# One core, a two-layer decoder step: the order of TensorE's instructions in the mixing stage

## The chip, the core and the metric

One core of a Trainium2 chip runs the whole program. The metric is the device time of one execution in microseconds (us). TensorE multiplies (its weight loads are listed apart, as PEld), VectorE (DVE), ScalarE (ACT) and GpSimd (POOL) do the elementwise work, and SyncE's queue (SP) issues nearly all DMAs. The kernel is written in a framework that takes the text of the program and then orders the instructions of each engine itself: it plays the program through with an own timing model and gives a free engine the earliest instruction of the text that is ready in that model. The order so made is fixed before the program runs; on the chip each engine works through its list.

## What is computed

Two layers, each with a SwiGLU block, a token mixing block and a second SwiGLU block, all with RMS norms. Tokens are 512 of a prompt and 8 x 8 of samples that continue a cache of 2048. The mixing block, cut to what matters:

```python
z = hn @ w_in_l                                   # 1024 -> 3584 = 28 items of 128 columns
aq, ak, av, bq, bf, bi, bg = split(z)             # attention q k v, then HGRN2 q f i g
outs = [dilated_window(aq, ak, av, w, d) for (w, d) in ((128, 1), (512, 4), (2048, 16))]
o_a = rmsnorm(dilated_mixture(outs), attn_g)      # softmax weights over three patterns
f = lb + (1 - lb) * sigmoid(bf);  qh = silu(bq)   # HGRN2, per head:
S_t = diag(f_t) S_{t-1} + (1 - f_t) outer i_t;  o_t = S_t^T qh_t
o_b = rmsnorm(o_t, hgrn_g) * silu(bg)
out = concat(o_a, o_b) @ w_out_l
```

The prompt starts its HGRN2 state at zero, the samples from a stored state; new keys, values and states are outputs too.

## The kernel before

Tokens lie in two halves of 288 columns (256 of the prompt, 32 of samples), `hf` 0 and 1. Every weight product is one **item** of 128 output columns; for each half it is 24 matmuls of 128 x 288 (8 tiles of the contraction, three products each, since weights and operands are split into a high and a low part; lines 353 to 355 in `product`). `run_phase` issues the items of a phase in order, both halves of an item one after the other in the mixing stage. `w_split` (lines 114 and 116) prepares weights ahead, `w_dma` (line 95) loads them.

The **mixing stage** (`mixing`) has 28 items of the input projection: 0 to 7 queries and keys, 8 to 11 values, 12 to 23 for HGRN2 head 0 to 3 in threes (forget gate, query, input), 24 to 27 the output gates. After each item and half, `evac` reads the product from PSUM and then `side` takes steps of the other work, all written as Python generators:

- `sample` (4 steps each time): attention of the samples, four pairs of sequences. Of each pair ten steps of scores (`sc`, line 849; each step reads two `kv` tiles of 256 KB that `kv_load`, lines 815 and 818, fetches into a ring of KVB = 5), one step with the new keys (`scn`) and the exponential (line 875), three of transposes (`ptps`, line 884), and for each sequence eleven products with the values (`pov`, line 904), a copy (line 910) and a transpose back (`otr`, line 913).
- `hgrn` (2 steps of each of up to two heads): eight steps of small products (`lev`, lines 590 to 631), after each of which DVE and POOL rescale `zq` and `zk` (lines 601, 639 to 661), which the next step reads; then `ktp`, `kv`, `pos`, `po`, `snew`, and the norm (`stat`, `bc`).
- `prompt` (2 steps): 16 units, each with four steps: scores (`psc`, line 765) and softmax, scaling, transposes (`ptp`, line 780, copied by ACT at line 784 and by DVE at line 782), product with the values (`ppv`, line 789).

PSUM has two buffers each for weight products (`ps_mm`), HGRN2 (`ps_hg`), samples (`ps_sa`) and prompt (`ps_pr`). Tiles of the pool `tmp` have six buffers; an output gate (items 24 to 27) holds one in the list `gates` until its head is done and `gate_outputs` uses it. Once the last item is there, `rest` goes round the generators until nothing is left, and `w_out` follows with eight items from another pool of PSUM. `rest` is also called from the middle of item 27's second half, by `hook` and `o_chain`.

The text thus says: 24 matmuls, then up to some ten small steps, then 24 matmuls, and so on. In which order TensorE takes them is the framework's choice: it may take a matmul of the next item while a step of a head waits for DVE.

Of the kernel before, what the change touches and what calls it, by code (L numbers as in the profile page):

```python
# [9 lines left out]

F32 = mybir.dt.float32
F32R = mybir.dt.float32r
U8 = mybir.dt.uint8
AF = mybir.ActivationFunctionType
ALU = mybir.AluOpType
# [32 lines left out]
def trunk_step(ctx: ExitStack, tc: tile.TileContext, a, L):  # L48
# [13 lines left out]
    ps_mm = ctx.enter_context(tc.tile_pool(name="ps_mm", bufs=2, space=PSUM))  # L62
    ps_hg = ctx.enter_context(tc.tile_pool(name="ps_hg", bufs=2, space=PSUM))

# [1 line left out]
    items = []  # L66
    for l in range(L):
        ff = {}
# [56 lines left out]
        while st["dma"] < min(st["split"] + 2, len(items)):  # L125
            w_dma()

# [1 line left out]
    def const(name, shape):  # L129
        return cp.tile(shape, F32, name=name)  # L130

# [34 lines left out]
    def late_consts():  # L166
        lstage = tmp("lstage")[:, :NLM * 32].rearrange("p (a b) -> p a b", b=32)
        for n, t in (("logits", logit), ("lmask", lstage), ("pbias", pbias), ("sb_str", sb_str), ("sb_rec", sb_rec),
                     ("sb_new", sb_new), ("bmask", bmask), ("eye32", eye32)):
            sp.dma_start(t if n == "lmask" else t[:], a[n])  # L170
        dve.tensor_copy(lmask[:], lstage)
        # lower bounds of the forget gates
        dve.tensor_copy(lbm[:], logit[:, 0, :])
        for l in range(1, L):
            dve.tensor_tensor(lbm[:], lbm[:], logit[:, l, :], op=ALU.max)
        for l in range(L):
            dve.tensor_tensor(lbe[:, l, :], logit[:, l, :], lbm[:], op=ALU.subtract)
        act.activation(lbe[:], lbe[:], AF.Exp)
        dve.tensor_copy(lbs[:], lbe[:, 0, :])
        for l in range(1, L):  # L180
            dve.tensor_tensor(lbs[:], lbs[:], lbe[:, l, :], op=ALU.add)
        dve.reciprocal(lbs[:], lbs[:])
        for l in range(L):
            dve.tensor_tensor(lbe[:, l, :], lbe[:, l, :], lbs[:], op=ALU.mult)
        dve.tensor_copy(lbm[:], lbe[:, 0, :])
        for l in range(L):
            if l:
                dve.tensor_tensor(lbm[:], lbm[:], lbe[:, l, :], op=ALU.add)
            dve.tensor_tensor(fof[:, l, :], lbm[:], lbe[:, 0, :], op=ALU.subtract)
            dve.tensor_scalar(fsc[:, l, :], fof[:, l, :], -0.5, 0.5, op0=ALU.mult, op1=ALU.add)  # L190
            dve.tensor_scalar(nfs[:, l, :], fsc[:, l, :], -1.0, None, op0=ALU.mult)
            dve.tensor_tensor(fof[:, l, :], fof[:, l, :], fsc[:, l, :], op=ALU.add)
# [2 lines left out]
    def tmp(name="tmp"):  # L195
        return tp.tile([P, H], F32, name=name, tag="tmp", bufs=6)

# [1 line left out]
    def stats(acc, inv, out_psum=False, tag="rb"):  # L199
        """rsqrt of the mean square of every token, on all partitions: [128, 288]"""  # L200
        s = ps_hg.tile([P, 512], F32, name="stat", tag="hg")
        for c in range(3):
            pe.matmul(s[:96, c:c + 1], acc[:, 96 * c:96 * c + 96], ones[:, 0:1], start=True, stop=True)
        sm = tp.tile([96, 4], F32, name="sm", tag="sm", bufs=2)
        dve.tensor_scalar(sm[:, :3], s[:96, :3], inv, EPS, op0=ALU.mult, op1=ALU.add)
        pool.tensor_tensor(sm[:, :3], sm[:, :3], nhalf[:96, :3], op=ALU.pow)  # L206
        yield
        b = ps_hg.tile([P, 512], F32, name="bc", tag="hg")
        for c in range(3):
            pe.transpose(b[:, 96 * c:96 * c + 96], sm[:, c:c + 1].to_broadcast([96, P]), ident[:96, :96])  # L210
        if out_psum:
            return b[:, :H]
        rb = tp.tile([P, H], F32, name="rb", tag=tag, bufs=1)
        act.activation(rb[:], b[:, :H], AF.Copy)
        return rb[:]

    class Chain:
        """what one half of the tokens goes through between two phases, issued in steps: jn tiles of the
        next operand are there, then its scale r"""

        def __init__(self, hf, gen):
            self.hf, self.jn, self.r, self.done = hf, 0, None, False
# [116 lines left out]
            c()  # L339

    def product(group, order=None, chain=None):
        """group: (psum, item, high, low); one tile of the contraction after the other, for all of them"""
        for _, i, _, _ in group:
            w_get(i)
        k = items[group[0][1]][1]
        order = order or range(k)
        for n, j in enumerate(order):
            s = slice(j * P, (j + 1) * P)
            if chain is not None:
                chain.until(n + 1)  # L350
            for ps, i, xhi, xlo in group:
                wh, wl = whi[i], wlo[i]
                pe.matmul(ps, wh[:, s], xhi[:, j, :], start=(n == 0), stop=False)  # L353
                pe.matmul(ps, wh[:, s], xlo[:, j, :], start=False, stop=False)  # L354
                pe.matmul(ps, wl[:, s], xhi[:, j, :], start=False, stop=(n == k - 1))  # L355
            if len(group) > 1 or n == k // 2 - 1:
                hook()

    def run_phase(n, operand, evac, chains, order=None, lag=LAG, side=None, on_done=None):
        """n items from items[st.next]; operand(i, hf) gives (psum, high, low), evac(i, hf, psum) takes the product"""  # L360
        i0 = st["next"]
        st["next"] += n

        def issue(idx, hf):
            group, tiles = [], []
            if idx[0] == 0:
                chains[hf].until(1)
            for i in idx:
                pst, xhi, xlo = operand(i, hf)
                group.append((pst[:, :H], i0 + i, xhi, xlo))  # L370
                tiles.append(pst)
            first = idx[0] == 0
            product(group, order if first else None, chains[hf] if first else None)
            flush_late()
            if hf == 0:
                w_ahead(i0 + idx[-1])
            else:
                w_ahead(i0 + idx[0])
            hook()
            if first:  # L380
                chains[hf].until_r()
            for i, pst in zip(idx, tiles):
                evac(i, hf, pst)
                if i == n - 1 and on_done is not None:
                    active.append(on_done(hf))
                if side is not None:
                    side(i, hf)

        g = list(range(GRP))
        issue(g, 0)  # L390
        issue(g, 1)
        for i in range(GRP, n):
            issue([i], 0)
            if i - lag >= GRP:
                issue([i - lag], 1)
        for i in range(max(GRP, n - lag), n):
            issue([i], 1)
        flush_late()

# [1 line left out]
    def swiglu(l, w, chains, gp, mk_chain, side=None):  # L401
        with ExitStack() as es:
            hpool = es.enter_context(tc.tile_pool(name="hid", bufs=1))
# [60 lines left out]
            run_phase(n, operand, evac, chains, side=side, on_done=on_done)  # L464
        return nxt

# [1 line left out]
    def mixing(l, chains, xpool_close, x_spill):  # L468
        o = [None, None]
        with ExitStack() as es:  # L470
# [39 lines left out]
            def evac(i, hf, pst):  # L510
                ps = pst[:, :H]
                r = rn[hf]
                if i < 8:
                    dst = (aq if i < 4 else ak)[:, i % 4, hf, :]
                    dve.tensor_tensor(dst, ps, r, op=ALU.mult)
                    if i == 7 and hf == 1:
                        late.append(lambda: sp.dma_start(a["o_k"][l], ak[:]))
                    return
                t = tmp("z")
                if i < 12 or (i < 24 and i % 3 == 2):  # L520
                    dve.tensor_tensor(t[:], ps, r, op=ALU.mult)
# [27 lines left out]
                    gates.append((h, hf, t))  # L549

            gates = []
            left = [12, 12]
            gated = [0, 0]
            normed = [False, False]
# [9 lines left out]
            hg_done = set()  # L564
            stage = [0] * 4

# [1 line left out]
            def pcol(t, c):  # L568
                return t[:, c // 2, (c % 2) * P:(c % 2) * P + P]

# [163 lines left out]
                hg_done.add(h)  # L734
                stage[h] = 4

# [1 line left out]
            def prompt_unit(p, i, alt):  # L738
                n = (i + 1) * P
                if alt == 1:  # L740
# [58 lines left out]
                    yield from prompt_unit(p, i, alt)  # L799
                    left[i // 2] -= 1  # L800

# [1 line left out]
            kvq = []  # L803
            kvs = {"n": 0}

# [132 lines left out]
            def side(i, hf):  # L938
# [10 lines left out]
                if i < 8:  # L949
                    return  # L950
                if i == 11 and hf == 1:
                    flush_late()
                    flags["av"] = True
                    prm.append(prompt(0))
# [17 lines left out]
                        if not pull(g):  # L972
                            hg.remove(g)

# [1 line left out]
            oa_g = g_of(l, "attn_norm_g")  # L976

            def anorm(hf):
# [43 lines left out]
            oc = [o_chain(0), o_chain(1)]  # L1022
            run_phase(28, operand, evac, chains, lag=0, side=side, on_done=lambda hf: oc[hf])
            tail["on"] = True
            while hg or prm or smp or alt or alt2 or an or gates:
                rest()
        return oc

    def w_out(l, chains, gp, mk_chain):
# [24 lines left out]
            run_phase(NJ, operand, evac, chains, on_done=on_done)  # L1054
        return nxt

# [1 line left out]
    xs = ExitStack()  # L1058

    def x_tiles():  # L1060
# [44 lines left out]
    xs.close()  # L1105


# [1 line left out]
def _tiles(w):  # L1109
    """(..., K, M) -> (..., M/128, 128, K): one contiguous [128, K/128 * 128] block for every 128 columns"""  # L1110
    *b, K, M = w.shape
    n = len(b)
    t = w.reshape(*b, K // P, P, M // P, P)
# [2 lines left out]


def _cols(v):
    """(L, n*128) -> (128, L, n)"""
    L = v.shape[0]  # L1120
    return np.transpose(v.reshape(L, -1, P), (2, 0, 1))

# [93 lines left out]
```

## Time and profile before

| | us |
|---|---|
| runs | 2618.42, 2623.82, 2625.37 (median 2623.82) |
| profiled execution, first to last instruction | 2620.2 |
| layer 0, item 12's first matmul to `w_out`'s first | 539.8 to 823.5 |
| layer 1, the same | 1837.5 to 2124.0 |

Busy times of TensorE add up the modelled lengths of overlapping matmuls (0.29 us each, one every 0.13 us), so a piece of work on it is best taken from start to start in the timeline. "idle before" in a row is time in which the engine had nothing to do, with the instruction that ended it. A weight matmul is 128 x 288; a name such as `sc<-kv,qbd` gives the tile written and those read, "x4" counts instructions merged into the row.

### The profile page before, as it was taken

How to read it: one execution, taken by the hardware profiler on the slowest of the kernel's cores; microseconds unless marked ns; L12 is line 12 of the kernel's file. 1: busy time of each engine (PE TensorE's matmuls, PEld its weight loads, DVE VectorE, ACT ScalarE, POOL GpSimd, SP SyncE). 2: the span in 40 equal slices, each digit the busy share in tenths (PEclk: the TensorE clock that was granted, in tenths of full speed). 3: DMA queues.
4: the chain of work that ended last, by engine and by line, in shares of the span. 5: the costliest groups of instructions: out<-in, count | busy, mean ns of one | idle time of the engine just before them, and what ended most of it. 6: DMA issues, size and time to landing. Idle time of an engine off the chain costs nothing.

```text
span 2620.2 us, 52041 instructions
## 1 busy us (share of the span) xinstructions
PE 2570.6 (98%) x21844; PEld 2401.9 (92%) x21844; DVE 1186.3 (45%) x2648; ACT 900.4 (34%) x2023; POOL 384.0 (15%) x450
## 2 busy tenths in 40 slices
PE   8999999999999999999999999999999999999997
PEld 8999999867878999999999999997677799999997
DVE  6333346235555642434563334362456556324333
ACT  5232235133335532223532322342333254323232
POOL 1101012002212210101210010110022122101012
PEclk9999999999999999999999999999999899999998
DMA  5222223475543222222222222236754442222221
GB/s 177 81 81 81 89 74 109 159 240 172 167 155 130 82 89 81 83 87 76 78 89 81 81 81 89 74 108 190 223 186 156 131 145 73 87 83 74 89 81 44
DMA packets 108604, 292.03 MB, mean 111 GB/s; under 512 B 12753, under 2 KB 16081, under 8 KB 107601
## 3 DMA queue, kind: packets, MB, share of 16 engines
q1 hardware_dynamic: 107936, 288.28, 34.0%
q8 instruction: 172, 2.82, 0.4%
q14 instruction: 64, 0.52, 0.1%
q10 hardware_dynamic: 432, 0.41, 0.1%
HBM read 272.13 MB, written 16.52 MB: 110 GB/s over the span
## 4 chain that ended last, share of the span: by engine, by line
PE 90%; DVE 4%; issue 3%; DMA 1%; POOL 1%; ACT 1%; SPq 0%; POOLq 0%; ACTq 0%; DVEq 0%
PE gu L353 13%; PE gu L354 13%; PE gu L355 13%; PE mm L353 12%; PE mm L355 12%; PE mm L354 12%; PE sc L849 2%; PE pov L904 1%; PE psc L765 1%; PE ppv L789 1%; DMA kv<-in_kc 1%; DVE y L313 1%; POOL sm L206 1%; PE ptp L780 1%; DVE x L316 1%
## 5 line engine op out<-in xcount | busy, mean ns | idle before, releaser
L353 PE MATMUL gu<-xh,whi 128*128 128x288 f32 x2752 | 813.3, 296 | 7.1 <-ACT xh L269 6.3
L354 PE MATMUL gu<-xl,whi 128*128 128x288 f32 x2752 | 813.1, 295 | 0.0
L355 PE MATMUL gu<-xh,wlo 128*128 128x288 f32 x2752 | 811.2, 295 | 0.0
L114 ACT ACTIVATE whi<-wraw 128x512 fp32r<-128x512 f32 (+1 forms) x688 | 394.9, 614 | 758.3 <-PE gu L354 360.6
L116 DVE TENSOR_TENSOR wlo<-wraw,whi 128x512 fp32r<-128x512 f32 (+1 forms) x688 | 445.3, 680 | 194.7 <-ACT whi L114 176.9
L353 PEld LDWEIGHTS gu<-xh,whi 128*128 128x128 f32 x2752 | 517.9, 188 | 8.3 <-ACT xh L269 6.7
L355 PEld LDWEIGHTS gu<-xh,wlo 128*128 128x128 f32 x2752 | 518.9, 189 | 0.0
L354 PEld LDWEIGHTS gu<-xl,whi 128*128 128x128 f32 x2752 | 517.7, 188 | 0.5 <-DVE xl L270 0.5
L353 PE MATMUL mm<-hh,whi 128*128 128x288 f32 x1408 | 415.7, 295 | 0.0
L355 PE MATMUL mm<-hh,wlo 128*128 128x288 f32 x1408 | 414.7, 295 | 0.0
L354 PE MATMUL mm<-hl,whi 128*128 128x288 f32 x1408 | 414.7, 295 | 0.0
L434 POOL TENSOR_TENSOR gate<-gate,rb 128x288 f32<-128x288 f32 x176 | 163.8, 931 | 1287.8 <-ACT gate L433 1287.8
L353 PE MATMUL mm<-xh,whi 128*128 128x288 f32 x1088 | 334.9, 308 | 1.5 <-DVE y L449 1.5
L354 PE MATMUL mm<-xl,whi 128*128 128x288 f32 x1088 | 327.3, 301 | 0.0
L355 PE MATMUL mm<-xh,wlo 128*128 128x288 f32 x1088 | 327.3, 301 | 0.0
L355 PEld LDWEIGHTS mm<-hh,wlo 128*128 128x128 f32 x1408 | 264.7, 188 | 0.0
L354 PEld LDWEIGHTS mm<-hl,whi 128*128 128x128 f32 x1408 | 264.4, 188 | 0.0
L353 PEld LDWEIGHTS mm<-hh,whi 128*128 128x128 f32 x1408 | 264.2, 188 | 0.0
L438 DVE TENSOR_TENSOR hid<-gu,gate 128x288 f32<-128x288 f32 x172 | 78.7, 457 | 332.2 <-PE gu L355 323.6
L353 PEld LDWEIGHTS mm<-xh,whi 128*128 128x128 f32 x1088 | 205.3, 189 | 25.1 <-issue 21.4
L354 PEld LDWEIGHTS mm<-xl,whi 128*128 128x128 f32 x1088 | 205.4, 189 | 12.9 <-issue 12.4
L355 PEld LDWEIGHTS mm<-xh,wlo 128*128 128x128 f32 x1088 | 205.6, 189 | 12.6 <-issue 12.1
(193 smaller groups left out, 2430.0 us busy)
## 6 DMA issues: line engine op xcount, KB each, us to landing
wraw<-in_wgu SPq DMA_DIRECT2D x175, 512.0 KB, 3.4
kv<-in_kc SPq DMA_DIRECT2D x160, 256.0 KB, 3.4
kv<-in_vc SPq DMA_DIRECT2D x160, 256.0 KB, 3.3
wraw<-in_wd SPq DMA_DIRECT2D x64, 448.0 KB, 3.3
wraw<-in_w_in SPq DMA_DIRECT2D x56, 512.0 KB, 4.2
wraw<-in_wd SPq DMA_DIRECT2D x32, 512.0 KB, 3.5
wraw<-in_w_out SPq DMA_DIRECT2D x16, 512.0 KB, 4.4
xs<-x SPq DMA_DIRECT2D x4, 1152.0 KB, 4.2
```

Of the source, the lines that this page charges most:

```text
L114: act.activation(whi[i][:, c], r[:, c], AF.Copy)
L116: dve.tensor_tensor(wlo[i][:, c], r[:, c], f(whi[i][:, c]), op=ALU.subtract)
L206: pool.tensor_tensor(sm[:, :3], sm[:, :3], nhalf[:96, :3], op=ALU.pow)
L313: ins = dve.tensor_tensor(y[:, js, :], y[:, js, :], rb[:, None, :].to_broadcast([P, 2, H]), op=ALU.mult)
L316: dve.tensor_tensor(x[:, js, :], x[:, js, :], y[:, js, :], op=ALU.add)
L353: pe.matmul(ps, wh[:, s], xhi[:, j, :], start=(n == 0), stop=False)
L354: pe.matmul(ps, wh[:, s], xlo[:, j, :], start=False, stop=False)
L355: pe.matmul(ps, wl[:, s], xhi[:, j, :], start=False, stop=(n == k - 1))
L434: pool.tensor_tensor(g[:], g[:], rn[hf], op=ALU.mult)
L438: dve.tensor_tensor(h[:], ps, gate[hf][:], op=ALU.mult)
L765: pe.matmul(dst, q, kk, start=True, stop=True, tile_position=(64 * s, 0))
L849: pe.matmul(ps[32 * p:32 * p + 32, c], qbd[:, 2 * bp + bb, p, :], rhs(p), start=(bb == 0), stop=(bb == 1), tile_position=(0, 32 * p))
```

## The change

A guard for the order by hand opens in `side` after item 11's second half and covers TensorE alone; it closes when the stage is done. What lies in it goes to TensorE's list in the order of the text. The other engines' lists, and TensorE's outside of it, are ordered as before. In `evac` an item from 24 on first runs `rest` while three or more gates wait in `gates`. Comments and docstrings are blanked. The core:

```diff
+END = 1
...
                 return
+                while i >= 24 and len(gates) >= 3:
+                    rest()
                 t = tmp("z")
...
             gates = []
+            man = ExitStack()
             left = [12, 12]
...
                 if i == 11 and hf == 1:
+                    man.enter_context(tc.manual_schedule(engines={mybir.EngineType.PE}))
                     flush_late()
                     flags["av"] = True
...
             tail["on"] = True
+            if END == 0:
+                man.close()
             while hg or prm or smp or alt or alt2 or an or gates:
                 rest()
+            man.close()
         return oc
```

## Rows read from the trace of the kernel before

**Rows 1.** The page, part 1: busy time of TensorE and of its weight loads.

```profile
PE 2570.6 (98%) x21844; PEld 2401.9 (92%) x21844; DVE 1186.3 (45%) x2648; ACT 900.4 (34%) x2023; POOL 384.0 (15%) x450
```

**Rows 2.** Stretches: length, busy time (count) by engine, clock, DMA share, GB/s.

```profile
539.80:823.50 283.70, 277.38 (x3332) 211.90 (x3332) 149.75 (x476) 97.52 (x281) 56.46 (x80) 0.99 0.52 167
1837.50:2124.00 286.50, 279.92 (x3332) 212.24 (x3332) 149.81 (x476) 97.52 (x281) 56.42 (x80) 0.98 0.51 166
```

**Rows 3.** Timeline of TensorE: first and last weight matmul of layer 0's stage.

```profile
539.77 0.40 PE L353 MATMUL mm<-xh,whi 128*128 128x288 f32 x1
...
823.36 0.30 PE L355 MATMUL mm<-xh,wlo 128*128 128x288 f32 x1
```

**Rows 4.** Timeline, TensorE and its weight loads: one kv tile between weight matmuls.

```profile
568.16 0.29 PE L355 MATMUL mm<-xh,wlo 128*128 128x288 f32 x1
568.29 0.29 PE L353 MATMUL mm<-xh,whi 128*128 128x288 f32 x1
568.51 0.63 PE L849 MATMUL sc<-kv,qbd 128*32 128x256 f32 x4
569.07 0.19 PEld L354 LDWEIGHTS mm<-xl,whi 128*128 128x128 f32 x1 [0.41 <-issue]
569.07 0.40 PE L354 MATMUL mm<-xl,whi 128*128 128x288 f32 x1
569.31 0.29 PE L355 MATMUL mm<-xh,wlo 128*128 128x288 f32 x1
569.43 0.30 PE L353 MATMUL mm<-xh,whi 128*128 128x288 f32 x1
```

**Rows 5.** Timeline of TensorE: four kv tiles together; prompt scores together and in halves.

```profile
561.29 1.07 PE L849 MATMUL sc<-kv,qbd 128*32 128x256 f32 x16
562.29 0.40 PE L355 MATMUL mm<-xh,wlo 128*128 128x288 f32 x1
...
599.39 0.70 PE L765 MATMUL psc<-ak,aq 64*128 64x256 f32 x4
600.02 0.40 PE L353 MATMUL mm<-xh,whi 128*128 128x288 f32 x1
...
653.32 0.70 PE L765 MATMUL psc<-ak,aq 64*128 64x256 f32 x2
653.94 0.67 PE L203 MATMUL stat<-ones,osq 128*96 128x1 f32 x6
654.54 0.70 PE L765 MATMUL psc<-ak,aq 64*128 64x256 f32 x2
655.17 0.40 PE L353 MATMUL mm<-xh,whi 128*128 128x288 f32 x1
```

**Rows 6.** Timeline: two steps of a head's levels, and what lies between them.

```profile
598.92 0.46 PE L590 MATMUL lev<-zq,zk 128*32 128x32 f32 x31
600.55 1.06 POOL L641 TENSOR_TENSOR zk<-zk,d 128x288 f32<-128x288 f32 x1
601.67 0.46 PE L590 MATMUL lev<-zq,zk 128*32 128x32 f32 x32 [0.99 <-DVE mx L768]
```

**Rows 7.** Timeline: new keys' scores of a sample pair, exponential, transposes.

```profile
584.57 0.39 PE L849 MATMUL scn<-ak,qbd 128*32 128x64 f32 x10
585.82 1.42 ACT L875 ACTIVATE ss<-ss,smx 128x1344 f32<-128x1344 f32 x1 [0.51 <-DVE smx L874]
588.45 1.04 PE L884 MATMUL ptps<-ident,ss 128*128 128x128 f32 x8
```

**Rows 8.** Groups by form: DVE and ACT copies behind ptp; copy behind pov.

```profile
L782 DVE COPY pt<-ptp 128x512 f32<-128x512 f32 x4 | 2.7, 684 | 0.5 <-PE ptp L780 0.5
L782 DVE COPY pt<-ptp 128x128 f32<-128x128 f32 x4 | 1.1, 287 | 0.9 <-PE ptp L780 0.9
L910 ACT ACTIVATE ob<-pov,smx 128x128 f32<-128x128 f32 x8 | 2.9, 362 | 1.4 <-issue 1.3
```

**Rows 9.** Line 815, layer 0's stage: time from issue to landing of kv.

```profile
DMA to landing us min/median/max: 2.5/3.6/5.8
```

**Rows 10.** Stretches: the three with a lower clock, columns as in rows 2.

```profile
630.40:633.80 3.40, 3.40 (x18) 3.40 (x18) 0.00 (x0) 1.11 (x5) 1.61 (x2) 0.50 0.61 196
804.50:807.90 3.40, 3.40 (x16) 2.65 (x15) 0.00 (x0) 0.96 (x5) 0.89 (x1) 0.50 0.02 5
2043.50:2057.20 13.70, 13.70 (x48) 7.91 (x47) 3.37 (x11) 3.49 (x10) 0.50 (x1) 0.50 0.42 137
```

## The prediction, made before the changed kernel was run

> **What bounds the kernel now.** I read the page's busy shares first, then the stretches, then TensorE's timeline. TensorE is busy 98% of the span [rows 1], so the time is what its list of instructions costs plus what it waits. Only the two mixing stages change, from item 12 on: 283.7 us in layer 0 and 286.5 us in layer 1, 570.2 us of the span's 2620.2 [rows 2]. In them TensorE is covered for 277.4 and 279.9 us: it hardly waits. The reader is to see that this is not the same as working at its best. The stage holds 32 half items of 24 weight matmuls, 768 from the first to the last one [rows 3]. A weight matmul follows another after 0.13 us, so 768 of them want 102 us; but the start of other work comes 0.22 us after the last one, and the second weight matmul 0.24 us after the first [rows 4]. A return trip so costs (0.22 - 0.13) + (0.24 - 0.13) = 0.20 us. In layer 0's timeline I count 88 pieces of weight matmuls: 102 + 88 x 0.20 = 120 us, which is what they take from start to start (120.7). The framework's order buys an engine without waits, and pays with small pieces. The change turns this round: large pieces, and waits.
>
> **The change, part by part.**
>
> *Pieces: a gain.* In text order 24 weight matmuls always stand together: 32 pieces in place of 88 a layer, 56 x 0.20 = 11 us less. A single kv tile between weight matmuls takes 0.56 us (568.51 to 569.07) [rows 4]; four together take 1.00 us, 0.25 each [rows 5]. The text takes two tiles a step and up to four steps together. The stage has 240 such matmuls, 60 tiles; they take 25.1 us from start to start and would take 60 x 0.25 = 15: 10 us less. Of the prompt's scores the two halves of a pair of heads take 0.63 us together, and 0.62 + 0.63 us apart [rows 5]; the text keeps them together in all 16 units. They take 20.2 us, and 13 if each unit stands whole: 7 us less. The same sum over the rest (ppv 3, ptp 2, pov 2, levels 2.5) gives 9, and 3 us of TensorE's present waits go. Together 40 us a layer, which leaves 285.1 (mean of the two stages) - 40 = 245 us of pure TensorE work.
>
> Here the Trainium skill speaks against the change: "TensorE: Matmul & The Clock Gate", section "What happens when you issue a matmul", says that TensorE loads the next tile's weights while the present matmul runs. By it a change of piece would cost next to nothing and the 11 us of the weight pieces would not be there. The trace disagrees: the load for the weight matmul at 569.07 begins at 569.07, after the samples' matmuls, though nothing else held it [rows 4]; so I keep the 0.20.
>
> *Waits: a loss.* In text order a step that waits for DVE, ACT, POOL or a DMA holds all that stands behind it in TensorE's list, the next 24 weight matmuls first, and with them the evacuation on DVE and the gate or z work on ACT and POOL behind that. Before, those matmuls filled such a wait. None of the waits is in the trace of before as such, so each is bounded from its chain.
> - Levels. `side` takes two steps of a head at once, and the second reads zk and zq which POOL and DVE rescale after the first. Four heads have four such pairs each, 16 a layer; some have another head's step between. From the first step's end (599.4) to the second's start (601.67) lie 2.2 us, with the POOL operation's 1.06 us in it [rows 6]. Low end 0.9 (POOL alone, a step of another head covering part of it), high end 2.2; I take 1.5, since DVE's copies come before its rescaling: 24 us (14 to 35).
> - Prompt. `ptp` and `ppv` stand in the same turn, and between them lies DVE's copy, 0.29 to 0.68 us [rows 8], plus the release of a PSUM buffer and of DVE. 16 units at 0.6 to 1.6, I take 1.1: 18 us (10 to 26).
> - kv tiles. A ring of five serves four score steps at once, eight tiles. The third step's second tile and the fourth's tiles are only requested when the first step has let go of its buffers, and land 2.5 us later at the least, 3.6 in the median [rows 9]; the second step covers some 0.5 us. Thirty score steps make about twelve such waits, at 1.0 to 2.4, I take 1.5: 18 us (12 to 29).
> - Exponential of the samples. From the end of `scn` to `ptps` lie 588.45 - 584.96 = 3.5 us [rows 7]; three pairs of sequences in the stage, 2.3 to 3.5 with 3.0 taken: 9 us (7 to 10).
> - `pov` to `otr`, the copy of 0.36 us [rows 8] and two signals, eight times 0.7: 6 us (4 to 10).
> - Others (`ktp` to `kv`, `stat` to `bc`, waits for a PSUM buffer): 8 us (5 to 8).
>
> Sum 83 us a layer (52 to 118). Net 83 - 40 = +43 a layer, +86 in both.
>
> *Queues.* No DMA is moved in the text; kv and weight loads stay on SP in the framework's order, and a later `sc` lets the kv loads start later, which is in the third term. POOL's list is short in the stage (56 us of 284) [rows 2] and hides nothing.
>
> *The cap on gates.* I followed the text: heads 0, 1 and 2 are done by item 25, `gate_outputs` runs in every `side`, so when item 26 or 27 comes at most two gates wait and the loop is never entered. Cost nothing. Were head 2 late by some half items, a few rounds of `rest` would stand before an evacuation, and they would have come later anyway.
>
> *The end.* Before, the last weight matmul of the stage starts at 823.36 and `w_out` begins right after [rows 3]. In the text `o_chain` puts the last four rounds of `rest` into the middle of item 27's second half, so twelve weight matmuls still stand behind the last norm. I cost the end at nothing; without that cover it is one norm chain, about 3 us a layer.
>
> **The sum.** 2620.2 + 86 = 2706 for the profiled execution. The median of the runs is 3.6 us above that span: 2710 us, 3.3% more.
>
> **The rivals.**
> - *Faster.* The waits come out short, because the other engines, which have half their time free [rows 2], finish while TensorE is on a neighbour's step of the same turn. The point is 40 us of waits a layer, half of what I take, 1.25 us a half item. With 28 us the stage is 12 us shorter, and the time 2624 - 24 = 2600. For it: the sum of pieces is well founded. Against it: my low ends already sum to 52, and each is a chain with nothing of its own turn to fill it.
> - *Clock.* The granted clock falls to 0.5, the lower level of 1.2 GHz, three times in the stages, for 3.4, 3.4 and 13.7 us [rows 10]; each time TensorE had just run 16 `pos` matmuls of 8 columns. In text order sparse steps and waits of some 7 us stand together between blocks of weights. Fell it in every second half item for 3.4 us, 16 x 3.4 = 54 us a layer would run at half speed, some 20 us lost: 2710 + 40 = 2750. The Trainium skill says it more sharply ("TensorE: Matmul & The Clock Gate", section "HAM oscillation"): waits between short bursts bring the clock down each time. By that every half item would be hit and 80 us lost, 2790; the trace so far shows single falls, so I leave the larger figure out of the sum.
> - *No change.* The framework's order is nearly the text's already, or the guard binds little: 2624. Against it: 88 pieces where the text has 32.
>
> **How the numbers follow.** Forecast 0.65, faster 0.20, clock 0.10, no change 0.05. The forecast's own range takes both ends of the waits: 52 - 40 = +12 and 118 - 40 = +78 a layer, 2648 to 2780; waits seldom all lie at one end, so 2655 to 2765. A range for 8 in 10 must take in half of the faster case: 2602 to 2770. A measurement of this kernel can tell some 0.3% from no change; by the cases, faster 0.20, same 0.05, slower 0.75.
>
> **What would show it.** Right: the two stages at about 328 us each and all else unchanged; 32 pieces of weight matmuls a layer with 3.2 us each; idle time of TensorE before `lev`, `ppv`, `sc`, `ptps` and `otr` with releasers DVE, ACT, POOL and kv, 80 us a layer in sum; weight matmuls never within a turn. Wrong: idle time below 40 us a layer, a clock below 0.95 in the stages, a change of time outside of them, or `rest` rounds before item 25's evacuation.

## The result, and the profile after

The changed kernel takes 2771.58 us (median; runs from 2764.71 to 2778.23) against 2624.6 us of the kernel before beside it: a ratio of 1.0569, 95% interval 1.0544 to 1.0595, 5.7% slower. The profiled execution spans 2762.9 us. The prediction had the sign and the waits, but no cost for the clock; it said +86 us, and +147 us came.

The page, part 1, of the kernel after, which answers to [rows 1]: TensorE falls from 98% to 94% of a longer span.

```profile
PE 2605.7 (94%) x21844; PEld 2443.1 (88%) x21844; DVE 1193.7 (43%) x2648; ACT 899.8 (33%) x2023; POOL 381.6 (14%) x450
```

The two stages of the kernel after, cut so that they hold 768 weight matmuls and end at `w_out`'s first, answering to [rows 2] with its columns (length, busy time and count by engine, granted clock, DMA share, GB/s):

```profile
535.40:890.30 354.90, 294.67 (x3338) 231.78 (x3336) 152.26 (x472) 98.12 (x282) 53.18 (x78) 0.88 0.41 134
1906.20:2262.80 356.60, 295.54 (x3336) 230.83 (x3336) 152.21 (x472) 98.18 (x282) 53.35 (x78) 0.88 0.41 134
```

Under the guard the two ends of this window are shifted by twelve matmuls: item 12's first starts only at 543.63, behind steps that now stand ahead of it, and item 27's last twelve start at 893.11, behind `w_out`'s first; the last twelve of item 11 lie inside in their place. This holds for all runs with the guard below. Cut from the end of item 11 to the end of item 27 instead, less the matmuls of `w_out` in between, layer 0's stage goes from 285.3 to 356.2 us: 70.9 us longer, where the window says 71.2.

Two things are to be seen. TensorE now is idle for 354.9 - 294.7 = 60.2 us of layer 0's stage, where it was 6.3 us; and its clock is 0.88 where it was 0.99. A mean of 0.88 means that 0.12 x 354.9 / 0.5 = 85 us ran at the lower level. Before, these were the single falls of [rows 10]; now there are 15 in each layer, of 3.4 to 13.7 us. Outside of the stages nothing moved: 2762.9 - 354.9 - 356.6 = 2051.4 us, and 2620.2 - 283.7 - 286.5 = 2050.0 before.

TensorE's timeline of the kernel after shows how the two go together (the bracket is the idle time before a row and what ended it):

```profile
578.02 0.29 PE L356 MATMUL mm<-xh,wlo 128*128 128x288 f32 x1
578.24 1.49 PE L853 MATMUL sc<-kv,qbd 128*32 128x256 f32 x20
581.57 1.32 PE L853 MATMUL sc<-kv,qbd 128*32 128x256 f32 x8 [1.84 <-DMA kv<-in_kc]
584.27 1.07 PE L853 MATMUL sc<-kv,qbd 128*32 128x256 f32 x4 [1.38 <-DMA kv<-in_kc]
585.27 0.69 PE L784 MATMUL ptp<-ident,S 128*128 128x128 f32 x2
...
587.62 0.44 PE L356 MATMUL mm<-xh,wlo 128*128 128x288 f32 x1
587.86 0.44 PE L354 MATMUL mm<-xh,whi 128*128 128x288 f32 x1
588.10 0.44 PE L355 MATMUL mm<-xl,whi 128*128 128x288 f32 x1
...
590.69 0.29 PE L354 MATMUL mm<-xh,whi 128*128 128x288 f32 x1
590.82 0.29 PE L355 MATMUL mm<-xl,whi 128*128 128x288 f32 x1
```

Five kv tiles run at once, as many as the ring holds; the other three come late, twice. The weight matmuls that follow are 0.24 us apart instead of 0.13, up to 590.5: the granted clock of this stretch is 0.5 (columns as above). Here the waits are paid twice, once in idle time, and once by the work behind them.

```profile
583.80:590.60 6.80, 6.11 (x25) 4.58 (x26) 0.90 (x3) 0.56 (x2) 0.00 (x0) 0.50 0.38 132
```

The waits of TensorE in layer 0's stage, by waiting line and releaser (us in total, times, longest):

```profile
PE sc L853 <- DMA kv<-in_kc: 15.6, 13, 2.6
PE ptps L888 <- ACT ss L879: 7.8, 3, 2.9
PE otr L917 <- ACT ob L914: 7.1, 8, 1.7
PE lev L635 <- DVE zq L663: 3.4, 3, 2.1
PE ppv L793 <- ACT pt L788: 3.2, 11, 0.3
PE lev L594 <- DVE s L730: 2.8, 3, 1.1
PE lev L594 <- POOL zk L645: 2.2, 1, 2.2
...
PE lev L594 <- DVE zq L605: 1.9, 2, 1.7
PE lev L635 <- POOL zk L665: 1.8, 3, 0.7
PE lev L594 <- POOL zk L665: 1.7, 3, 0.6
...
PE ppv L793 <- DVE pt L786: 1.5, 6, 0.5
...
PE lev L594 <- DVE zq L663: 1.3, 1, 1.3
PE lev L594 <- DVE sm L206: 1.3, 3, 0.7
```

All eight rows of `lev` together make 16.4 us. Before, the waits for kv tiles made 2.0 us in the same stage, all of `lev` 2.2 and `otr` behind ACT 0.2. The largest rows are all named in the prediction.

### The profile page after: what moved, and what is told of

The parts are those of the page before. It is cut to its first block, busy times and chain, and to the rows that moved or that the text cites. A ratio compares the mean times of both kernels' runs of the same rounds, so it can differ in the third digit from the quotient of the medians.

```text
span 2762.9 us, 52005 instructions
## 1 busy us (share of the span) xinstructions
PE 2605.7 (94%) x21844; PEld 2443.1 (88%) x21844; DVE 1193.7 (43%) x2648; ACT 899.8 (33%) x2023; POOL 381.6 (14%) x450
## 5 line engine op out<-in xcount | busy, mean ns | idle before, releaser
L354 PE MATMUL mm<-xh,whi 128*128 128x288 f32 x1088 | 345.6, 318 | 1.6 <-DVE y L450 1.5
L355 PE MATMUL mm<-xl,whi 128*128 128x288 f32 x1088 | 335.5, 308 | 0.0
L356 PE MATMUL mm<-xh,wlo 128*128 128x288 f32 x1088 | 333.3, 306 | 0.0
L354 PEld LDWEIGHTS mm<-xh,whi 128*128 128x128 f32 x1088 | 217.3, 200 | 27.7 <-issue 24.4
L355 PEld LDWEIGHTS mm<-xl,whi 128*128 128x128 f32 x1088 | 217.3, 200 | 6.3 <-issue 6.2
L356 PEld LDWEIGHTS mm<-xh,wlo 128*128 128x128 f32 x1088 | 216.8, 199 | 2.5 <-issue 2.5
```

## The experiments

Theory **W**: what the written order loses are the waits of steps that follow one another in one turn of `side`, and the low clock that comes with them. Theory **C**: the low clock comes from the rows of small matmuls themselves, packed between blocks of weights, whether or not TensorE waits in them. "Low clock" below is the sum of the stretches with a granted clock of 0.5 in a stage, "idle" its length less TensorE's covered time. The kernel before lay at 2617 to 2620 us beside these runs; ratios are to it.

**The same steps in two turns.** With the guard kept, half of the steps come after 12 of an item's 24 weight matmuls and half after all of them, so that twelve weight matmuls lie between two steps of one generator.

```diff
+            if n == 3 and st.get("mid"):
+                st["mid"]()                    # in product
...
+            def turn():
+                pull_all(smp, 2)
+                pull_hg(1)
+                pull_all(prm, 1)
...
-                pull_all(smp, 4)
-                pull_hg(2)
-                pull_all(prm, 2)
+                turn()
```

> The text order stays, but the steps that belonged to one half item are taken in two turns: two sample steps, one step of each head and one prompt step after the first 12 weight matmuls, the same again after all 24. Theory W (waits of TensorE's in-order list, and the low clock that these waits bring with them, are all of the loss): each dependent pair now has 12 weight matmuls (1.6 us) between its two steps, so of the 83 us of waits a layer some 15 remain and the low clock nearly goes; 33 more pieces cost 33 x 0.2 = 7 us; a stage of 245 + 7 + 15 = 267 us where it is 355, so 2771 - 176 = 2595 us, under the kernel before. Theory C (the low clock comes from the small matmuls in a row themselves, waits or not, and is the larger part): low clock stays near 60 us a layer, a stage near 300 us, 2660 us.

Measured: 2625.73 us, ratio 1.0027 (1.0013 to 1.0041). The stretches of its stages:

```profile
537.10:820.70 283.60, 261.67 (x3337) 207.52 (x3335) 151.33 (x473) 97.58 (x281) 56.73 (x78) 0.97 0.52 168
1837.10:2123.60 286.50, 264.68 (x3336) 210.64 (x3336) 151.58 (x473) 98.22 (x282) 57.72 (x78) 0.95 0.51 168
```

Idle falls from 60 to 22 us a layer and low clock from 85 to 17 and 27: 140 us of the loss are gone, with every matmul still in the order of the text and 64 pieces of weights. The time lies between the two theories: the low clock is far under the 60 us of C, but 22 us of waits are left where W had 15, and the stages are 17 to 20 us longer than W's 267. Three terms that turns of half the size can't part make most of what is left; its waits show them:

```profile
PE otr L919 <- ACT ob L916: 6.8, 8, 2.2
PE ptps L890 <- ACT ss L881: 6.3, 3, 2.1
PE sc L855 <- DMA kv<-in_kc: 4.3, 7, 1.9
```

**The same turn, woven.** Nothing is taken earlier or later than by a turn, but the steps of a turn alternate: a head, two of the samples, the prompt, and again.

```diff
-                pull_all(smp, 4)
-                pull_hg(2)
-                pull_all(prm, 2)
+                for _ in range(2):
+                    pull_hg(1)
+                    pull_all(smp, 2)
+                    pull_all(prm, 1)
```

> The text order stays and the weight matmuls stay in pieces of 24; only within a turn the steps are woven: one step of each head, two sample steps, one prompt step, and all that once more. Theory W: between the two steps of a dependent pair now lie about 1.2 us of other steps, so the waits of levels and of ppv fall by about 1 us each, 32 x 1.0 = 32 us a layer, the kv waits stay; a stage of about 320 us, 2700 us. Theory C: the row of small matmuls is as long as before, the clock stays as low (85 us a layer), and the gain is at most half of that: 2735 us.

Measured: 2655.16 us, ratio 1.0156 (1.0141 to 1.0171), better than both theories said. The stages:

```profile
535.50:835.80 300.30, 267.76 (x3336) 214.62 (x3336) 145.87 (x472) 97.06 (x280) 53.49 (x78) 0.93 0.49 158
1853.10:2156.70 303.60, 269.41 (x3337) 216.51 (x3336) 145.99 (x472) 97.12 (x280) 53.56 (x78) 0.93 0.48 157
```

The weights still stand in 33 pieces of 24, between them equally long rows of small matmuls; what has halved are the waits (33 us) and with them the low clock (41 and 44 us). That speaks against C.

**Half of the kv tiles.** Each pair of tiles that a score step reads becomes one tile read twice; half of the keys of the samples' cache are left out, 80 of the 320 loads of both layers together (40 of 160 a layer; the expectation below counts them as one layer's).

```diff
-                                t = [kvq.pop(0), kvq.pop(0)]
+                                t = [kvq.pop(0)] * 2
...
-                                kv_load()
```

> The changed kernel with half of the keys of the sample cache left out: a score step reads one kv tile for both of its uses, so that the ring of five holds the tiles of four steps and 80 of 320 loads of each layer's ring go. Theory W: the kv waits of the stage (18 us estimated, 40 us by the idle rows of the weight loads and matmuls of the scores) go, with their share of the low clock: a stage of 320 to 330 us, 2700 to 2720 us. If the scores' waits only hide another wait that then comes to light (levels and prompt steps stand right behind them), less than 8 us a layer: above 2755 us.

Measured: 2684.71 us, ratio 1.0268 (1.0253 to 1.0283). The stages, and the group of the score matmuls (count, busy time, mean ns, idle before):

```profile
531.60:851.30 319.70, 274.50 (x3298) 223.03 (x3296) 151.38 (x472) 98.11 (x282) 53.21 (x78) 0.91 0.36 117
...
L853 PE MATMUL sc<-kv,qbd 128*32 128x256 f32 x240 | 15.0, 382 | 0.0
```

The 15.6 us of waits are gone and the stage is 35 us shorter, at the 320 us that W had said (the time is 15 us under W's 2700, 8 us of them outside of the stages). Low clock fell from 85 to 55 us, which at the price found below is 13 us; the rest is that the score matmuls, no longer torn up by waits, take 14.0 us from start to start, where they took some 22 at the full clock and without their waits. These waits are worth more than their length: here 35 us for 15.6.

**Useless matmuls in the waits.** Ahead of the steps that wait, matmuls of 128 x 256 on operands that are there, their result overwritten: 358 a layer in the first run, 180 in the second.

```diff
+            def warm_up(ps, n, c=0):
+                for _ in range(n if hot["on"] else 0):
+                    pe.matmul(ps[:, c:c + 256], hot["x"][:, 0, :P], hot["x"][:, 1, :HP], start=True, stop=True)
...
                     ps = ps_hg.tile([P, 512], F32, name="lev", tag="hg")
+                    warm_up(ps, n)
```

(In the same way before `ppv`, before `sc` in a turn's third and fourth step, `ptps` and `otr`.)

> The changed kernel with additional matmuls of 128 x 256 (results overwritten by what follows) placed just ahead of the steps that wait: 8 ahead of every second level, 12 ahead of the last one, 3 ahead of ppv, 10 ahead of the third or fourth score step of a turn, 18 ahead of the sample transposes, 4 ahead of otr. Nothing that is waited for comes earlier; TensorE is busy while it waits. Theory W: the waits hide the additional work but for some 8 us a layer, the low clock falls from 85 to under 30 us a layer and gives some 25 us back: 2771 - 2 x 17 = 2737 us. Theory C: the clock is the larger part, 45 us a layer come back less the 8: 2695 us. If the clock has no part in it: slower, 2790 us.

> The changed kernel with useless matmuls ahead of the steps that wait, about half as many as in the run with full filling (there: 27 to 34 us a layer at the low clock in place of 85, the weight matmuls 109 us in place of 122, and yet 349 us a layer, as the filling overran the waits). Theory W and its clock part (low clock costs half its length): filling that mostly fits into the waits costs 5 to 10 us a layer, the low clock falls to 40 to 60 us and gives 12 to 22 back: stages of 335 to 345 us, 2735 to 2755 us. Theory C (rows of small matmuls bring the clock down, whether or not TensorE waits): low clock near 85 us and 2775 us or more.

Measured: 2749.85 us, ratio 1.0513 (1.0496 to 1.053), with 358; 2759.85 us, ratio 1.0546 (1.0527 to 1.0564), with 180. So 358 matmuls more a layer make the program *shorter* than the changed kernel (1.0569), by some 15 us as the ratios say and by 10.7 us in the two stages of the profiles, although they overrun the waits. With 180 the difference lies within the intervals. Both runs are slower than W had said, by 5 to 13 us, and neither fits C. Stages, first of the run with 358, then of that with 180:

```profile
535.60:884.60 349.00, 318.76 (x3695) 256.46 (x3694) 149.84 (x472) 98.52 (x282) 53.15 (x78) 0.96 0.42 137
1898.70:2250.50 351.80, 321.06 (x3696) 258.68 (x3694) 149.93 (x472) 98.04 (x281) 53.18 (x78) 0.95 0.41 136
```

```profile
537.00:878.50 341.50, 303.60 (x3518) 239.16 (x3516) 149.58 (x472) 98.61 (x282) 52.90 (x78) 0.95 0.43 140
1895.30:2258.80 363.50, 324.41 (x3517) 257.88 (x3515) 149.87 (x472) 99.05 (x282) 53.07 (x78) 0.88 0.40 133
```

With 358, the 768 weight matmuls of a layer take 108.5 and 110.2 us from start to start, 122.4 in the changed kernel's layer 0. The second run gave more than it was made for. Its two layers have the same instructions and nearly the same idle time (37.9 and 39.1 us), yet one has 37.5 us at the low clock and the other 85.3, and TensorE is covered 20.8 us longer. So **a microsecond at the low clock costs 20.8 / 47.8 = 0.44 us**, measured within one execution. Between the two layers of other runs the same division gives 0.3 to 0.5, from differences of only 3 to 10 us at the low clock. And the run limits theory W: neither the list nor the waits alone fix the low clock, since here the same list with nearly the same waits has it twice as long. What decided between the two layers stays open.

**Apart also the last pairs.** To the run with two turns one pause is added in `sample`, so that `pov`'s copy and `otr`, and `scn` and `ptps`, fall into different turns; and the same text without the guard.

```diff
+                            if kt == 10 and bp == 0 and bb == 0:
+                                yield
```

> The two-turn text with one more pause in the mixing stage, so that the copy of pov on ScalarE and its transposes, and the sum scn and its transposes, fall into different turns. In the two-turn version 7.3 us a layer were idle ahead of the output's transposes and 6.5 us ahead of scn's, of 23.5 us of waits, with 17 and 27 us at the low clock. Theory W (what is lost to the written order are the waits and the low clock that follows them): waits of 8 to 12 us a layer, low clock of 8 to 17 us, stages of 270 us and about 2595 us in all, faster than the kernel before by about 1%. Theory C (the low clock comes from the rows of small matmuls, whether or not they wait): low clock as in the two-turn version, stages of 277 us, about 2612 us.

> The text of the run with the extra pause, with TensorE's order left to the framework again. If a gain of that run comes from the order of TensorE as written, this one is at the kernel before (2610 to 2625 us, some 88 weight pieces a layer); if it comes from the way in which the steps are now handed out, this one is as fast as that (about 2595 us).

Measured: 2596.17 us, ratio 0.9913 (0.99 to 0.9927), with the guard; 2597.61 us, ratio 0.9921 (0.9904 to 0.9937), without it. The stages, first with the guard, then without:

```profile
536.90:805.10 268.20, 257.64 (x3337) 203.32 (x3335) 152.09 (x473) 95.08 (x277) 53.82 (x75) 0.99 0.56 178
1826.90:2091.20 264.30, 255.88 (x3337) 203.30 (x3336) 151.88 (x473) 95.13 (x277) 53.65 (x75) 0.99 0.56 181
```

```profile
540.20:806.50 266.30, 261.89 (x3320) 204.91 (x3320) 152.56 (x474) 95.44 (x278) 55.07 (x76) 0.99 0.56 177
1826.80:2093.70 266.90, 262.47 (x3321) 204.76 (x3321) 152.56 (x474) 95.70 (x279) 55.58 (x77) 0.99 0.56 177
```

The guard is not what gains: the text is. Handed out in halves, the steps make larger pieces for the framework too (`psc` 21 pieces of 29, `ppv` 17 of 27, `ptp` 16 of 24, 337 pieces of all kinds in place of 362), and it waits less (4.4 us) than the written order (10.6 and 8.4), which in turn has 64 pieces of weights in place of 81. Over the whole run these two differences cancel. (With the guard item 27's last twelve matmuls and the last norm's waits come behind the window; cut at the end of item 27 as above, its stages are 273.9 and 269.9 us, and 267.9 and 268.4 without it.) Both runs are faster than the kernel before by 0.8 to 0.9%, the first at the 2595 us that W had said.

**The end brought forward.** Both runs lost 12 to 14 us outside of the stages (2063.8 and 2062.3 us against 2050.0). In the run without the guard the timeline after the stage has two waits for the last norm, with thirteen weight matmuls at half speed behind them:

```profile
809.62 0.67 PE L204 MATMUL stat<-ones,acc 128*96 128x1 f32 x6 [1.99 <-POOL acc L261]
...
811.99 0.46 PE L211 MATMUL bc<-ident,sm 96*128 96x96 f32 x3 [0.97 <-POOL sm L207]
```

```diff
+            def turn_end():
+                turn()
+                pull_all(an, 1)
+                gate_outputs()
...
+                if i == 25 and hf == 0:
+                    st["mid"] = turn_end
                 if i == 27 and hf == 0:
                     st["mid"] = None
+                    turn_end()
```

> The run with the framework's order and steps in two turns, with the end of the stage brought forward: from item 25 on each turn also takes a step of the norm and of the gates, and the last one is a whole turn. In that run the part of the span outside of the stages was 12 us longer than before (2062 against 2050): after the stage, w_out's matmuls waited 2.0 and 1.0 us for the last norm's chain on POOL, and 3.4 us of them ran at the low clock. If that chain is the 12 us, the stages stay at 267 us, the rest is back at 2050 to 2055 and the time is about 2586 us. If the steps that are now taken earlier wait inside the stage instead, the time stays at 2596 us.

Measured: 2596.14 us, ratio 0.992 (0.9904 to 0.9935): no gain. The rest is back at 2054.1 us, but the stages have grown to 267.1 and 273.3 us. Layer 0's has the norm's wait inside now (below), and layer 1's has 10.2 us of low clock and 8.0 us of idle time (7 and 4 in the run before). The wait was moved, not covered.

```profile
802.37 0.46 PE L211 MATMUL bc<-ident,sm 96*128 96x96 f32 x3 [1.37 <-POOL sm L207]
```

**The runs side by side**, us a layer:

| | stage | idle | low clock |
|---|---|---|---|
| before | 283.7, 286.5 | 6, 7 | 7, 14 |
| changed | 354.9, 356.6 | 60, 61 | 85, 85 |
| half of the kv tiles | 319.7, 319.7 | 45, 45 | 55, 55 |
| woven turn | 300.3, 303.6 | 33, 34 | 41, 44 |
| two turns | 283.7, 286.5 | 22, 22 | 17, 27 |
| two turns and a pause | 268.2, 264.3 | 11, 8 | 7, 7 |
| the same, framework's order | 266.3, 266.9 | 4, 4 | 7, 7 |
| the same, end brought forward | 267.1, 273.3 | 6, 8 | 0, 10 |
| 358 useless matmuls | 349.0, 351.8 | 30, 31 | 27, 34 |
| 180 useless matmuls | 341.5, 363.5 | 38, 39 | 38, 85 |

Where the idle time is over 20 us, the low clock is 0.8 to 1.4 times as long in all stages but one (180 useless matmuls, layer 1: 2.2 times); where it is under 12 us, the low clock is 0 to 14 us.

## Why the prediction was right in sign and too small in size

Layer 0's stage grew by 71.2 us; the prediction's net was +43. By terms:

- **Idle time: +54, predicted +80** (83 of new waits less 3 of old). The list of waits was right: 13 waits for kv tiles (12 predicted, 15.6 us for 18), 3 for the exponential (7.8 for 9), 8 of `otr` (7.1 for 6), the levels (16.4 for 24) and the prompt (4.7 for 18). The last two were oversized. Of the levels' 16.4 us 4.1 stand behind `s` and `sm`; before the rescaled `zq` and `zk` there are 13 waits for the 16 predicted, of 0.9 us in the mean and not 1.5 (the first answer to [rows 6] in the trace after is 1.68 us). Between `ptp` and `ppv` TensorE idles 0.2 to 0.5 us a time and not 1.1: I had added signals and a buffer's release to the copy of [rows 8], and the traces show no more than the copies.
- **Low clock: +35, predicted 0.** (85.3 - 6.8) x 0.44 = 34.5 us, an estimate that carries the price over from another run. This is the step that failed. I had the mechanism, half speed after rows of sparse steps, and had it as a *rival* of the waits with a chance of 0.10. The two don't exclude one another: in the experiments the low clock shrinks with the waits, so its price belonged into the forecast's sum. The rival's 54 us a layer were too low as well; 85 came. Nor does a row of `pos`, which the prediction saw ahead of each fall, bring one by itself: of the eight rows of `pos` in the two stages before, five are followed by none. On the Trainium skill's "TensorE: Matmul & The Clock Gate", section "HAM oscillation — how this bites in real kernels", the prediction had set a figure of 80 us for both layers aside. The trace comes near that figure in the sum, 2 x 85.3 x 0.44 = 75 us, but not in the way: there are 15 falls a layer, not one in each of the 32 half items. That section of the Trainium skill prices time at the lower clock at half of its length, and the 0.44 here is near.
- **Pieces: -17, predicted -37.** What remains: 71.2 - 53.9 - 34.5 = -17. Where TensorE ran at the full clock I took each kind of matmul from start to start without the idle time, and scaled up to all of its kind. The weights fall from 118.6 to 107.8 us, 11 as said, so the 0.20 a return trip of [rows 4] stands; `psc` falls from 19.5 to 12.2, 7 as said. But `sc` falls only from 24.0 to 21.8 (10 were predicted), and `ppv`, `ptp`, `pov` and `lev` don't fall at all: from 15.3, 10.3, 23.0 and 16.1 to 17.9, 11.9, 23.8 and 17.2. The second step that failed is that I took a gain of [rows 5] for pieces that my own list of waits tears up: the score row of the timeline above is `x20`, `x8`, `x4` and not one `x32`. Where those waits are gone most sizes come: in the run with two turns and a pause, `ppv` takes 11.1, `ptp` 8.3 and `lev` 14.6 us, and without the kv waits `sc` takes 14.0; in the former `sc` (22.1) and `pov` (25.5) still gain little or nothing. Over all kinds of matmul this second way of counting gives a gain of 10 to 14 us and not 17, so the split between low clock and pieces is good to some 5 us.

Together the misses are -26 + 35 + 20, rounded, +28 a layer (71.2 - 43), and the two layers, with 1.4 us outside of them, make the 57 us between the predicted span of 2706 and 2762.9. That the sum came as near as it did is in part luck: the oversized waits hid some of the clock and the pieces.

The other steps held. The stretch outside of the stages stayed (2051.4 us), so the end cost nothing. The cap on gates does nothing: with the bound raised from three to nine, the lists of all five engines are the same, as the reading of the text had said. 33 pieces of weights came for 32; the middle of item 27's second half makes the one more. Of the rivals, *faster* needed less than 40 us of waits a layer; 60 came. With some 10 us of waits a layer, in the run with two turns and a pause, the written order does beat the kernel before, but the framework's order of the same text is as fast, so that gain is not the order's. Of the signs named as "wrong", the clock below 0.95 in the stages is the one that appeared.

## What to carry to other kernels

On an engine that is busy all the time, an order by hand buys larger pieces and pays for each wait, so count the waits first: hand out the steps such that a step and the one that reads its result never fall into one turn, and only then judge the order. Then price each wait above its length: in this kernel the stage without the 15.6 us of waits for kv tiles was 35 us shorter, as its score matmuls stood together and less of it ran at the low clock. And before keeping an order by hand, run its text with the framework's order: here the text made the whole gain and the guard none.

## What the hardware showed that was not expected

- Idle times of at most 2.9 us, among rows of small matmuls, came with a granted clock of 0.5 for 85 us of a 355 us stage in which TensorE was covered 83% of the time.
- The same list in two layers of one execution had 37.5 and 85.3 us at the low clock, and the stages took 341.5 and 363.5 us: a stage's time can differ by 6% with nothing in the list and little in the waits to show for it.
- Useless matmuls in waits paid for themselves: 358 more a layer, and the ratio to the kernel before fell from 1.0569 to 1.0513, some 15 us.
